# RMSNorm with gamma and Silu on one core: a ring of 24 rows with uneven blocks in place of six equal buffers

## The chip, the cores and the metric

The kernel runs on one core of a Trainium2 chip. The metric is the device time of one execution in microseconds (us). The kernel before was run four times: its median is 316.83 us, the lowest run 316.7 us and the highest 317.09 us.

## What is computed

```python
x = np.random.randn(8, 1024, 2048).astype(np.float32)
gamma = np.random.randn(2048).astype(np.float32)
eps = np.float32(1e-5)

rms = np.sqrt(np.mean(x ** 2, axis=-1, keepdims=True) + eps)
out = gamma * x / rms
return (out * (1 / (1 + np.exp(-out)))).astype(np.float32)
```

The input is 8192 rows of 2048 float32 numbers, 67.11 MB, and the output has the same size. Each row is squared and summed, multiplied by the reciprocal of its root mean square and by gamma, and put through Silu.

## The kernel before

**Tiling.** The 8192 rows are cut into 16 blocks of 512 rows. A block lies in SBUF as 128 partitions of 4 rows (J = 4), each partition's 4 rows being 32 KB that are contiguous in HBM. So the whole problem is 64 "rows per partition" in and 64 out, and below "row" always means one such row over all 128 partitions (1 MB). There are six buffers of 4 rows each (BUFS = 6): 24 rows, 192 KB a partition. All arithmetic is in place: a block is loaded into its buffer, worked on there, and stored from there.

**Queues.** `load` (L52 to L55) issues a block's load from the ScalarE queue (ACTq in the profile; its DMA queue is q10). `store` (L101, L102) issues a block's store from the SyncE queue (SPq; DMA queue q1). Both run on the same 16 DMA engines. The six loads that fill the buffers are issued at the start (L106, L107). A later load, of block b+3, is issued on ScalarE inside the squares of block b+1 (L67 to L69), and goes into the buffer of block b-3, so it waits for that block's store. A store waits for the last Silu of its block.

**Work of a block.** `squares_scalar` squares and sums the first one or two rows on ScalarE (L65, result thrown into PSUM, the sum kept), `squares_vector` the other two or three on VectorE (L73). `root` is a Sqrt on ScalarE with scale and bias (L82), `invert` the reciprocal on VectorE (L87). `multiply` makes x times rstd times gamma in one VectorE instruction for each row (L92). `silu` runs Silu over two rows at a time (L98) and then issues the store.

**Order.** The order of instructions is written out by hand. For most blocks (b from 3 to 13) the squares and the root of block b+1 stand ahead of the product and Silu of block b: a look-ahead of one block. The last block (L149 to L156) is done another way: gamma times x needs no rstd, so the two first products stand ahead of the reciprocal (L152), and the Silu takes rstd as its scale, one row at a time (L154).

**Start.** Gamma is loaded into one partition by SyncE, spread to 128 partitions by TensorE (L114) and copied to SBUF (L115).

Of the kernel before, what the change touches and what calls it, by code (L numbers as in the profile page):

```python
# [1 line left out]

# [4 lines left out]

ACT = mybir.ActivationFunctionType
ALU = mybir.AluOpType


@with_exitstack
def kernel(
    ctx: ExitStack,
    tc: tile.TileContext,
    x: bass.AP,
    gamma: bass.AP,
    eps: bass.AP,
    out: bass.AP,
):  # L20

    nc = tc.nc
    P = nc.NUM_PARTITIONS
    f32 = mybir.dt.float32
    x2 = x.flatten_outer_dims()
    o2 = out.flatten_outer_dims()  # L30
    n, d = x2.shape
    J = 4
    BUFS = 6
    nblk = n // (P * J)
    xb = x2.rearrange("(b p j) d -> b p (j d)", p=P, j=J)
    ob = o2.rearrange("(b p j) d -> b p (j d)", p=P, j=J)

    singles = ctx.enter_context(tc.tile_pool(name="singles", bufs=1))
    pool = ctx.enter_context(tc.tile_pool(name="pool", bufs=BUFS))
    small = ctx.enter_context(tc.tile_pool(name="small", bufs=2))  # L40
    psum = ctx.enter_context(tc.tile_pool(name="psum", bufs=1, space=bass.MemoryType.PSUM))

    Q = 4
    w = d // Q
    g = singles.tile([P, d], f32)
    eps_t = singles.tile([P, 1], f32)
    ones = singles.tile([P, P], f32)
    junk_a = psum.tile([P, d], f32, name="junk_a")
    junk_v = psum.tile([P, d], f32, name="junk_v")
    blocks, sss, rmss, rstds = {}, {}, {}, {}  # L50

    def load(b):  # L52
        xt = pool.tile([P, J * d], f32, name="xt")
        nc.scalar.dma_start(out=xt, in_=xb[b])  # L54
        blocks[b] = xt  # L55

    def row(b, j):
        return blocks[b][:, j * d:(j + 1) * d]

    def squares_scalar(b, loads=()):  # L60


        sss[b] = small.tile([P, J], f32, name="ss")
        for j in range(share(b)):
            nc.scalar.activation(out=junk_a, in_=row(b, j), func=ACT.Square,  # L65
                                 accum_out=sss[b][:, j:j + 1])
            if j == 0:  # L67
                for s in loads:
                    load(s)  # L69

    def squares_vector(b):
        for j in range(share(b), J):
            nc.vector.tensor_tensor_reduce(  # L73
                out=junk_v, in0=row(b, j), in1=row(b, j), scale=1.0, scalar=0.0,
                op0=ALU.mult, op1=ALU.add, accum_out=sss[b][:, j:j + 1])

    def share(b):
        return 1 if 4 <= b <= 12 and b % 2 == 0 else 2

    def root(b):  # L80
        rms = small.tile([P, J], f32, name="rms")
        nc.scalar.activation(out=rms, in_=sss.pop(b), func=ACT.Sqrt, scale=1.0 / d, bias=eps_t)  # L82
        rmss[b] = rms

    def invert(b):
        rstd = small.tile([P, J], f32, name="rstd")
        nc.vector.reciprocal(out=rstd, in_=rmss.pop(b))  # L87
        rstds[b] = rstd

    def multiply(b):  # L90
        for j in range(J):
            nc.vector.scalar_tensor_tensor(out=row(b, j), in0=row(b, j), scalar=rstds[b][:, j:j + 1],  # L92
                                           in1=g, op0=ALU.mult, op1=ALU.mult)

    def silu(b):
        for h in range(0, J, 2):
            cols = slice(h * d, (h + 2) * d)
            nc.scalar.activation(out=blocks[b][:, cols], in_=blocks[b][:, cols], func=ACT.Silu)  # L98
        store(b)

    def store(b):  # L101
        nc.sync.dma_start(out=ob[b], in_=blocks[b])  # L102

    with tc.manual_schedule():

        for b in range(BUFS):  # L106
            load(b)  # L107
        nc.vector.memset(ones, 1.0)  # L108
        nc.vector.memset(eps_t, float(eps))
        nc.scalar.activation(out=junk_a[:, 0:1], in_=ones[:, 0:1], func=ACT.Square)  # L110
        nc.sync.dma_start(out=g[0:1, :], in_=bass.AP(tensor=gamma.tensor, offset=gamma.offset, ap=[[d, 1], [1, d]]))
        for c in range(Q):
            cols = slice(c * w, (c + 1) * w)
            nc.tensor.matmul(junk_v[:, cols], ones[0:1, :], g[0:1, cols], start=True, stop=True)  # L114
        nc.vector.tensor_copy(out=g, in_=junk_v)  # L115

        last = nblk - 1
        SOON = 3  # L120
        squares_scalar(0)
        squares_vector(0)
        root(0)
        invert(0)
        for b in range(last):
            loads = [b + 3] if BUFS <= b + 3 < nblk else []
            if b < SOON:
                multiply(b)
                squares_scalar(b + 1, loads)
                silu(b)  # L130
                squares_vector(b + 1)
                root(b + 1)
            elif b < last - 1:
                squares_scalar(b + 1, loads)
                squares_vector(b + 1)
                root(b + 1)
                multiply(b)
                silu(b)
            else:
                multiply(b)  # L140
                squares_scalar(b + 1)
                silu(b)
                squares_vector(b + 1)
                root(b + 1)
            if b + 1 < last:
                invert(b + 1)


        for j in range(J):  # L149
            if j == J // 2:  # L150
                invert(last)
            nc.vector.tensor_mul(out=row(last, j), in0=row(last, j), in1=g)  # L152
        for j in range(J):
            nc.scalar.activation(out=row(last, j), in_=row(last, j), func=ACT.Silu,  # L154
                                 scale=rstds[last][:, j:j + 1])
        store(last)  # L156


# [1 line left out]
_INS = ['x', 'gamma', 'eps']  # L160
_OUTS = [((8, 1024, 2048), 'float32')]

_NUMBERS = {'eps': 9.999999747378752e-06}


# [26 lines left out]
```

## Time and profile before

| what | value |
|---|---|
| median of four runs | 316.83 us |
| the profiled execution's own time | 317.07 us |
| span that the profile shows of it | 315.3 us |
| VectorE busy | 235.3 us, 75% of the span |
| ScalarE busy | 213.7 us, 68% of the span |
| bytes moved by DMA | 134.24 MB, mean 426 GB/s |
| time that DMA packets took, as a share of 16 engines' span | q10 (loads) 49.8%, q1 (stores) 49.3% |
| median time from issue to landing | loads 38.7 us, stores 29.3 us |

The page gives busy times by engine, then the span in 40 slices with the DMA engines' share and rate in each, the DMA queues, the chain of work that ended last, and the groups of instructions by line. In a group "x60 | 137.0, 2345 | 0.1" says 60 instructions, 137.0 us busy in all, 2345 ns each, and 0.1 us of idle time ahead of them. A DMA "packet" in these counts is either one partition's 32 KB of a block or the four bytes that report a DMA engine's end to a semaphore: a block's DMA has 128 of the first and 16 of the second, 8 and 1 on each of the 16 DMA engines.

### The profile page before, as it was taken

How to read it: one execution, taken by the hardware profiler on the slowest of the kernel's cores; microseconds unless marked ns; L12 is line 12 of the kernel's file. 1: busy time of each engine (PE TensorE's matmuls, PEld its weight loads, DVE VectorE, ACT ScalarE, POOL GpSimd, SP SyncE). 2: the span in 40 equal slices, each digit the busy share in tenths (PEclk: the TensorE clock that was granted, in tenths of full speed). 3: DMA queues.
4: the chain of work that ended last, by engine and by line, in shares of the span. 5: the costliest groups of instructions: out<-in, count | busy, mean ns of one | idle time of the engine just before them, and what ended most of it. 6: DMA issues, size and time to landing. Idle time of an engine off the chain costs nothing.

```text
span 315.3 us, 437 instructions
## 1 busy us (share of the span) xinstructions
PE 7.2 (2%) x8; PEld 2.5 (1%) x8; DVE 235.3 (75%) x157; ACT 213.7 (68%) x136; POOL 0.2 (0%) x4
## 2 busy tenths in 40 slices
PE   6200000000000000000000000000000000000000
PEld 2000000000000000000000000000000000000000
DVE  0579597979995695957969489693996929999600
ACT  1349998972799258782687727876278768779910
POOL 0000000000000000000000000000000000000000
DMA  8999999999999999999999999999999999999996
GB/s 329 416 449 424 403 437 403 466 399 466 399 467 399 463 403 461 403 461 403 461 412 453 416 449 424 445 424 441 432 432 432 432 449 412 457 407 457 407 457 279
DMA packets 4612, 134.24 MB, mean 426 GB/s; under 512 B 513, under 2 KB 513, under 8 KB 513
## 3 DMA queue, kind: packets, MB, share of 16 engines
q10 hardware_dynamic: 2304, 67.11, 49.8%
q1 hardware_dynamic: 2306, 67.12, 49.3%
q14 instruction: 2, 0.02, 0.0%
HBM read 67.12 MB, written 67.11 MB: 426 GB/s over the span
## 4 chain that ended last, share of the span: by engine, by line
DMA 68%; DVE 14%; ACT 11%; issue 2%; ACTq 1%; DVEq 0%
DMA xt<-in_x_dram 68%; DVE xt L92 9%; DVE junk_v L73 5%; ACT xt L98 4%; ACT junk_a L65 3%; ACT xt L154 2%; ACT L82 1%; ACTq L187 1%; ACT L154 0%; ACT L98 0%; ACT rms L82 0%; DVE ss L73 0%; DVE rstd L87 0%; ACTq L54 0%; ACTq L82 0%
## 5 line engine op out<-in xcount | busy, mean ns | idle before, releaser
L92 DVE SCALAR_TENSOR_TENSOR xt<-xt,rstd,g 128x2048 f32<-128x2048 f32 x60 | 137.0, 2345 | 0.1
L98 ACT ACTIVATE xt<-xt 128x4096 f32<-128x4096 f32 x30 | 108.3, 3615 | 27.1 <-DVE xt L92 27.1
L73 DVE CUSTOM_DVE_ANT_0 junk_v<-xt 128x2048 f32<-128x2048 f32 x37 | 85.1, 2299 | 42.9 <-DMA xt<-in_x_dram 42.2
L65 ACT ACTIVATE junk_a<-xt 128x2048 f32<-128x2048 f32 x27 | 50.7, 1876 | 23.1 <-DMA xt<-in_x_dram 22.8
L82 ACT ACT_TABLE_LOAD x15 | 19.2, 1283 | 27.4 <-DVE ss L73 27.3
L98 ACT ACT_TABLE_LOAD x14 | 18.0, 1283 | 0.2
L115 DVE COPY g<-junk_v 128x2048 f32<-128x2048 f32 x1 | 2.3, 2291 | 9.1 <-PE junk_v L114 9.1
L87 DVE RECIPROCAL rstd<-rms 128x4 f32<-128x4 f32 x16 | 2.7, 172 | 8.3 <-ACT rms L82 8.3
L152 DVE TENSOR_TENSOR xt<-xt,g 128x2048 f32<-128x2048 f32 x4 | 8.9, 2278 | 0.0
L82 ACT ACTIVATE rms<-ss,eps_t 128x4 f32<-128x4 f32 x16 | 4.8, 297 | 5.7 <-DVE ss L73 5.5
L154 ACT ACTIVATE xt<-xt,rstd 128x2048 f32<-128x2048 f32 x4 | 7.7, 1990 | 0.0
L114 PE MATMUL junk_v<-g,ones 1*128 1x512 f32 x8 | 7.2, 1072 | 2.9 <-DMA g<-in_gamma_dram 2.9
L73 DVE DVE_READ_ACCUMULATOR2_ANT ss<- 128x1 f32 x37 | 5.2, 140 | 0.0
L65 ACT ACTIVATION_READ_ACCUMULATOR junk_a<-xt 128x1 f32 x27 | 5.0, 186 | 0.0
L110 ACT ACT_TABLE_LOAD x1 | 1.3, 1283 | 3.8 <-issue 3.8
L114 PEld LDWEIGHTS junk_v<-g,ones 1*128 1x128 f32 x8 | 2.5, 327 | 6.0 <-issue 6.0
L154 ACT ACT_TABLE_LOAD x1 | 1.3, 1283 | 0.0
L108 DVE MEMSET ones<- 128x128 f32 x1 | 0.2, 165 | 0.8 <-PEq L173 0.8
L110 ACT ACTIVATE junk_a<-ones 128x1 f32<-128x1 f32 x1 | 0.2, 174 | 0.0
L173 POOL MEMSET const-bfloat16-1.0<- 128x1 bf16 x1 | 0.1, 103 | 0.0
L173 POOL MEMSET const-uint8-127<- 128x1 uint8 x1 | 0.1, 103 | 0.0
L173 POOL MEMSET const-float32-1.0<- 128x1 f32 x1 | 0.1, 100 | 0.0
(2 smaller groups left out, 0.2 us busy)
## 6 DMA issues: line engine op xcount, KB each, us to landing
xt<-in_x_dram ACTq DMA_DIRECT2D x16, 4096.0 KB, 38.7
out_dram<-xt SPq DMA_DIRECT2D x16, 4096.0 KB, 29.3
g<-in_gamma_dram SPq DMA_DIRECT2D x1, 8.0 KB
```

The costliest lines, as they stand in the source:

```text
L65: nc.scalar.activation(out=junk_a, in_=row(b, j), func=ACT.Square, accum_out=sss[b][:, j:j + 1])
L73: nc.vector.tensor_tensor_reduce(out=junk_v, in0=row(b, j), in1=row(b, j), scale=1.0, scalar=0.0, op0=ALU.mult, op1=ALU.add, accum_out=sss ...
L82: nc.scalar.activation(out=rms, in_=sss.pop(b), func=ACT.Sqrt, scale=1.0 / d, bias=eps_t)
L87: nc.vector.reciprocal(out=rstd, in_=rmss.pop(b))
L92: nc.vector.scalar_tensor_tensor(out=row(b, j), in0=row(b, j), scalar=rstds[b][:, j:j + 1], in1=g, op0=ALU.mult, op1=ALU.mult)
L98: nc.scalar.activation(out=blocks[b][:, cols], in_=blocks[b][:, cols], func=ACT.Silu)
L110: nc.scalar.activation(out=junk_a[:, 0:1], in_=ones[:, 0:1], func=ACT.Square)
L114: nc.tensor.matmul(junk_v[:, cols], ones[0:1, :], g[0:1, cols], start=True, stop=True)
L115: nc.vector.tensor_copy(out=g, in_=junk_v)
L152: nc.vector.tensor_mul(out=row(last, j), in0=row(last, j), in1=g)
L154: nc.scalar.activation(out=row(last, j), in_=row(last, j), func=ACT.Silu, scale=rstds[last][:, j:j + 1])
L187: with _tile.TileContext(nc) as tc:
```

## The change

The six buffers become one ring tile of 24 rows per partition. The 64 rows are cut into 12 blocks of 4, 4, 6, 4, then seven times 6, then 4 rows; a block of 6 rows is 48 KB a partition, contiguous in HBM. The first five blocks fill the ring (4 + 4 + 6 + 4 + 6 = 24); from there blocks 5 to 10 go to the places 0, 6, 12, 18, 0 and 6, and block 11 to place 12. Load i+2 is issued on ScalarE behind the first Silu row of block i, for i from 3 to 9; it waits for the stores of the blocks whose rows it overwrites, the youngest of which is block i-2.

Each block is done by itself, with no instruction of the next one between: half its rows squared on ScalarE and half on VectorE, the root, then gamma products of two rows at a time with no rstd in them (the reciprocal behind the first pair), then Silu by rows with rstd as scale, then the store. On VectorE the order is: the block's squares, first pair, reciprocal, other pairs, and then the next block's squares. On ScalarE: the block's squares, Sqrt, all its Silu rows, and then the next block's squares. The first pair of products overwrites rows that ScalarE squares, so it waits for those squares.

```diff
-    J = 4
-    BUFS = 6
-    nblk = n // (P * J)
-    xb = x2.rearrange("(b p j) d -> b p (j d)", p=P, j=J)
-    ob = o2.rearrange("(b p j) d -> b p (j d)", p=P, j=J)
+    RING = 24
+    sizes = [4, 4, 6, 4] + [6] * 7 + [4]
+    R = max(sizes)
+    nblk = len(sizes)
+    starts, places = [], []
+    row, place = 0, 0
+    for k in sizes:
+        if place + k > RING:
+            place = 0
+        starts.append(row)
+        places.append(place)
+        row, place = row + k, place + k
+    first = next(i for i in range(1, nblk) if places[i] == 0)
+
+    def block(t, i):
+        lo, k = starts[i] * P, sizes[i]
+        return t[lo:lo + k * P, :].rearrange("(p r) d -> p (r d)", r=k)
...
-    pool = ctx.enter_context(tc.tile_pool(name="pool", bufs=BUFS))
+    ring = singles.tile([P, RING * d], f32)
...
+    def rows(i, lo, hi):
+        return ring[:, (places[i] + lo) * d:(places[i] + hi) * d]
+
+    def load(i):
+        nc.scalar.dma_start(out=rows(i, 0, sizes[i]), in_=block(x2, i))
+
+    def store(i):
+        nc.sync.dma_start(out=block(o2, i), in_=rows(i, 0, sizes[i]))
+
+    def compute(i):
+        k = sizes[i]
+        mid = k // 2
...
+        for r in range(mid):
+            nc.scalar.activation(out=junk_a, in_=rows(i, r, r + 1), func=ACT.Square,
+                                 accum_out=ss[:, r:r + 1])
+        for r in range(mid, k):
             nc.vector.tensor_tensor_reduce(
-                out=junk_v, in0=row(b, j), in1=row(b, j), scale=1.0, scalar=0.0,
-                op0=ALU.mult, op1=ALU.add, accum_out=sss[b][:, j:j + 1])
+                out=junk_v, in0=rows(i, r, r + 1), in1=rows(i, r, r + 1), scale=1.0, scalar=0.0,
+                op0=ALU.mult, op1=ALU.add, accum_out=ss[:, r:r + 1])
+        nc.scalar.activation(out=rms[:, 0:k], in_=ss[:, 0:k], func=ACT.Sqrt, scale=1.0 / d, bias=eps_t)
+        for r in range(0, k, 2):
+            if r == 2:
+                nc.vector.reciprocal(out=rstd[:, 0:k], in_=rms[:, 0:k])
+            two = rows(i, r, r + 2).rearrange("p (r d) -> p r d", r=2)
+            nc.vector.tensor_mul(out=two, in0=two, in1=g.unsqueeze(1).to_broadcast([P, 2, d]))
+        for r in range(k):
+            row = rows(i, r, r + 1)
+            nc.scalar.activation(out=row, in_=row, func=ACT.Silu, scale=rstd[:, r:r + 1])
+            if r == 0 and i + 2 in range(first, nblk):
+                load(i + 2)
+        store(i)
...
-        for b in range(BUFS):
-            load(b)
+        for i in range(first):
+            load(i)
...
-        last = nblk - 1
-        SOON = 3
-        squares_scalar(0)
-        squares_vector(0)
-        root(0)
-        invert(0)
-        for b in range(last):
...
-        store(last)
+        for i in range(nblk):
+            compute(i)
```

More of the change, by code (lines that the diff above doesn't have):

```diff
@@ L49 @@
     junk_v = psum.tile([P, d], f32, name="junk_v")
[L50 to L69, printed above, removed]
@@ L71, in squares_vector @@
-    def squares_vector(b):
-        for j in range(share(b), J):
-            nc.vector.tensor_tensor_reduce(
-                out=junk_v, in0=row(b, j), in1=row(b, j), scale=1.0, scalar=0.0,
-                op0=ALU.mult, op1=ALU.add, accum_out=sss[b][:, j:j + 1])
[L77 to L99, printed above, removed]
@@ L101, in store @@
-    def store(b):
-        nc.sync.dma_start(out=ob[b], in_=blocks[b])
+    def rows(i, lo, hi):
[7 more added lines that the diff above has]
+        mid = k // 2
+        ss = small.tile([P, R], f32, name="ss")
+        rms = small.tile([P, R], f32, name="rms")
+        rstd = small.tile([P, R], f32, name="rstd")
+        for r in range(mid):
+            nc.scalar.activation(out=junk_a, in_=rows(i, r, r + 1), func=ACT.Square,
+                                 accum_out=ss[:, r:r + 1])
+        for r in range(mid, k):
+            nc.vector.tensor_tensor_reduce(
+                out=junk_v, in0=rows(i, r, r + 1), in1=rows(i, r, r + 1), scale=1.0, scalar=0.0,
[12 more added lines that the diff above has]
+        store(i)
@@ L112 @@
         for c in range(Q):
-            cols = slice(c * w, (c + 1) * w)
-            nc.tensor.matmul(junk_v[:, cols], ones[0:1, :], g[0:1, cols], start=True, stop=True)
+            nc.tensor.matmul(junk_v[:, c * w:(c + 1) * w], ones[0:1, :], g[0:1, c * w:(c + 1) * w],
+                             start=True, stop=True)
         nc.vector.tensor_copy(out=g, in_=junk_v)
-        last = nblk - 1
-        SOON = 3
-        squares_scalar(0)
-        squares_vector(0)
-        root(0)
-        invert(0)
-        for b in range(last):
[L126 to L155, printed above, removed]
-        store(last)
+        for i in range(nblk):
+            compute(i)
 _INS = ['x', 'gamma', 'eps']
```

## The prediction

> **What bounds the kernel now.** I read the page's engine shares and DMA slices first, then the DMA queues, the chain that ended last, and the DMA queues in short stretches. First the page:
>
> ```profile
> PE 7.2 (2%) x8; PEld 2.5 (1%) x8; DVE 235.3 (75%) x157; ACT 213.7 (68%) x136; POOL 0.2 (0%) x4
> ...
> DMA  8999999999999999999999999999999999999996
> ...
> q10 hardware_dynamic: 2304, 67.11, 49.8%
> q1 hardware_dynamic: 2306, 67.12, 49.3%
> ```
>
> No compute engine is near full, while the DMA engines are busy in every slice but the first and last: loads and stores together fill 99.1% of them. Taken over one stretch, from the first bytes to the last:
>
> ```profile
> 1.20:312.90 311.70, 7.16 (x8) 2.50 (x8) 235.12 (x155) 213.74 (x136) 0.00 (x0) 1.00 1.00 431
> ```
>
> The last three columns are clock, DMA share and GB/s: share 1.00. So 311.7 of the 315.3 us are DMA without a hole, 1.2 us lie ahead and 2.4 behind. Every idle time of an engine is slack under that. The chain agrees: 68% of it is a load, and its ScalarE and VectorE pieces lie beside busy DMA engines.
>
> Next, how fast DMA goes and how two queues share it. From the timeline (start, duration, then what ended the idle time):
>
> ```profile
> 13.26 1.88 ACT L65 ACTIVATE junk_a<-xt 128x2048 f32<-128x2048 f32 x1 [8.04 <-DMA xt<-in_x_dram]
> 13.31 2.30 DVE L73 CUSTOM_DVE_ANT_0 junk_v<-xt 128x2048 f32<-128x2048 f32 x1 [0.93 <-DMA xt<-in_x_dram]
> ...
> 22.89 1.88 ACT L65 ACTIVATE junk_a<-xt 128x2048 f32<-128x2048 f32 x1 [3.16 <-DMA xt<-in_x_dram]
> ...
> 24.92 1.88 ACT L65 ACTIVATE junk_a<-xt 128x2048 f32<-128x2048 f32 x1
> ```
>
> Blocks 0 and 1 land 9.63 us apart: 8 packets on each DMA engine, 1.204 us each. Later, with both queues busy (the chain's loads from 104.72 to 182.35), two blocks in and two out take some 38.8 us, 1.21 us a packet. Now the queues in one microsecond and in the next:
>
> ```profile
> q1 hardware_dynamic: 10, 0.33, 75.8%
> q10 hardware_dynamic: 6, 0.20, 45.5%
> ...
> q10 hardware_dynamic: 10, 0.33, 75.8%
> q1 hardware_dynamic: 6, 0.20, 45.5%
> ```
>
> Ten packets take 75.8% of 16 us: 1.213 us each, as long as a packet of loads alone (143 of them, 127 of 32 KB, fill 100.4% of 16 engines from 13.2 to 22.8 us). A packet isn't stretched by the other queue; each engine serves one packet of one queue, then one of the other. This matters below, since the change makes packets of 48 KB and of 32 KB.
>
> **The change, part by part.**
>
> *Bytes and DMAs.* The bytes stay: 64 rows in, 64 out. The DMAs go from 32 to 24; on each DMA engine 256 data packets become 64 of 32 KB and 128 of 48 KB. A 48 KB packet is in no row. If a packet's time is all bytes, it takes 1.82 us and the sum is unchanged: 0. If the 9 ns between 1.213 and 1.204 are a fixed cost, 64 packets fewer save 0.6 us. On the other side, the nearest row of a DMA loss is where stores first join the loads:
>
> ```profile
> 35.00:38.00 3.00, 0.00 (x0) 0.00 (x0) 0.96 (x2) 2.97 (x4) 0.00 (x0) 1.00 1.26 481
> 38.00:42.00 4.00, 0.00 (x0) 0.00 (x0) 4.00 (x3) 3.95 (x5) 0.00 (x0) 1.00 0.75 279
> ```
>
> Mean (3x481 + 4x279)/7 = 366 GB/s against 432: 1.1 us lost, once. Were such a loss paid at each of the eight places where a queue goes from one packet size to the other or starts, it would be 8.8 us; nothing shows that size is its cause. I take -0.3, the middle of the two nearer ends, and keep +2.2 (two such losses) for the range.
>
> [...]
>
> *Engine work.* VectorE loses the 60 products with rstd (137.0 us) and gets 32 products of pairs, each by the two-row stretch of L152 4.5 us: 32 x 4.5 = 144, where 137.0 + 8.9 stood. Silu by rows is 64 x 1.92 (7.68/4 of L154) = 123 where 108.3 + 7.7 stood. Table loads go from 31 to 25, 1.28 each. All of it is under the DMA as long as no queue runs dry, so its cost is 0; what it costs without that cover depends on how long a block takes, without look-ahead:
>
> - Block ready, ScalarE frees last: squares of rows 0 and 1, 2 x 2.03 (13.26 to 15.29 is one) = 4.1; first pair 4.5, for it overwrites those rows; reciprocal 0.2 (Sqrt and its table load end before); then one pair (4 rows) or two (6 rows) of 4.5; two Silu 3.9. Sum 17.2 for 4 rows, 21.7 for 6.
> - Block just landed: VectorE's own squares come first, 2.39 each (13.31 to 15.70): 4.8 or 7.2 in place of 4.1, sums 17.9 and 24.8.
>
> DMA needs 6 x 2 x 2.42 = 29.1 us for six rows in and out, so the engines keep up. What the look-ahead hid is now latency between landing and store; who notices is the store queue, if it is empty then.
>
> *Does a queue run dry?* I follow the packets, 8 per block and engine (1.213 or 1.82), one from each queue in turn, 1.2 us from last packet to landing.
> - Store 0 is issued at 13.3 + 4.8 + 4.5 + 0.2 + 4.5 + 3.9 = 31.2 (before: 35.4) and starts near 32.4. Block 2's last 2.1 packets pass with 2.1 of it: 2.1 x 3.03, to 38.8.
> - Block 3, 8 x 2.43, to 58.2. Store 0 ends at 53.1; store 1 is issued at 31.2 + 17.2 = 48.4, 4.7 ahead.
> - Block 4 beside store 1's last 5.9 packets, 5.9 x 3.03, to 76.1; store 2 came at 48.4 + 21.7 = 70.1, 6.0 ahead. Then 2.1 x 3.64: block 4 ends at 83.7.
> - Load 5 needs store 1 (77.3) and Silu row 0 of block 3 (about 80): in time for 83.7. Loads 5 and 6 end at 111.6 and 137.1 by the same steps, stores 2 and 3 at 105.2 and 129.5.
> - From there all blocks have 6 rows, 8 x 3.64 = 29.1 us each. Load i+2 goes out when store i-2 has landed, some 6 us before the load ahead of it ends.
> - End: load 10 ends at 253.6, load 11 at 277.9. Then stores run alone: 9 to 288.6, 10 to 303.2, 11 to 312.9. Store 10 is ready at 253.6 + 1.2 + 24.8 = 279.6, store 11 at some 297.5: 9 and 6 us ahead.
>
> No gap: DMA ends at 312.9 as before.
>
> *The added wait.* Load i+2 stands on ScalarE behind the first Silu row and waits there for store i-2: block 6's Silu begins at 138.3 + 7.2 + 4.5 + 0.2 = 150.2, store 4 lands at 158.6 + 1.2. Behind it on ScalarE wait five Silu rows (9.8 us) and the block's store, ready at 169.6, while store 5 runs until 187.7. Cost 0. If store 5 were gone by then, DMA would still have the load.
>
> Sum: 315.3 + 0 - 0.3 = 315.0 us of span. The profiled run took 317.07, 0.24 over the median; the same 0.3 off the median gives 316.5.
>
> [...]
>
> **Rivals.**
> *1. Sharing by bytes* (slower). If 48 KB goes out at half rate beside 32 KB, the early 6-row loads lose their larger share, loads end later and fewer stores are left to cover the last blocks. From 32.4 on 51.6 rows remain to load at 4.84: to 282.1. Load 10 lands near 263.9, store 10 is issued at 288.7, while store 9 has ended at 282.1 + 2.4 x 2.42 = 287.9: with 1.3 to start 2.1 us idle. It ends at 304.5; store 11 comes at 288.7 + 17.2 + 1.3 = 307.2: 2.7 idle. Sum +4.8: 321.3. It decides once store 10 or 11 comes after its predecessor's end. For it: no row shows packets of two sizes. Against it: the packets' unstretched 1.213 us. Chance 0.14.
> *2. Size-change losses* (slower): two more of the 1.1 us losses, 316.5 + 2.2 = 318.7. The one loss seen is at a change of the mix, but the last change, to stores alone near 280, shows none. 0.10.
> *3. The wait on ScalarE drains both queues.* Each of some six steady blocks would pay the start of a load, 12.4 (first load, issue to landing) - 9.7 = 2.7: +16, 333. The 6 us and 18 us of cover above speak against it. 0.04.
> *4. Larger packets pay* (faster): the whole 0.6 and part of the 38-to-42 loss, together 1.1: 315.7. Against it: 1.204 is already reached with 32 KB. 0.12.
>
> **How the numbers follow.** The forecast, DMA without a hole, has 0.60, own range 315.9 to 317.4. About 0.2%, 0.63 us, is what a measurement here can tell from no change: of the 0.60, 0.06 is faster and 0.02 slower than that. Faster 0.06 + 0.12 = 0.18, same 0.52, slower 0.02 + 0.14 + 0.10 + 0.04 = 0.30. The range goes from 315.2 (rival 4 and its lower half) to 320.4 (rival 2, and rival 1 with part of its idle time); about 0.17 is left out, nearly all above.
>
> **What would show it.** DMA share 1.00 from 1.2 to 312.9 again; store 0 issued near 31.2; 48 KB packets of 1.82 us; loads ended near 278 and last store issued near 297. Wrong: a DMA hole near 288 or 305 (rival 1), loads ended after 281, or a rate below 425 GB/s in slices with both queues busy (rival 2).

## The result, and the profile after

| | kernel before | changed kernel |
|---|---|---|
| median | 316.93 us (62 runs) | 317.36 us (43 runs) |
| lowest and highest run | 316.70 and 317.19 us | 316.88 and 319.46 us |
| the profiled execution: time, span | 317.07, 315.3 us | 317.13, 315.3 us |

The changed kernel takes 1.0019 times as long, with a 95% interval of 1.0015 to 1.0024: some 0.6 us more, where 0.3 us less was forecast (the ratio is one of means; the medians are 0.43 us apart). The time lies inside the stated range of 315.2 to 320.4 us; what came out the other way is the direction. Two things stand out. The loss is small but certain, and the changed kernel scatters over 2.6 us where the kernel before scatters over 0.5 us. The profiled execution happens to be one of its quicker runs, with the same span as before, so it shows the course of the kernel well and the loss badly; the loss is looked for in the other profiles below.

The page after, with the lines that were shown of before:

```profile
PE 7.2 (2%) x8; PEld 2.5 (1%) x8; DVE 217.1 (69%) x111; ACT 222.9 (71%) x166; POOL 0.2 (0%) x4
...
DMA  8999899999999999999999999999999999999996
...
q10 hardware_dynamic: 1728, 67.11, 49.6%
q1 hardware_dynamic: 1730, 67.12, 49.2%
```

VectorE has 18 us less to do and ScalarE 9 us more, and DMA is busy in every slice as before. The same bytes go in 25% fewer packets (64 data packets fewer and 8 end marks fewer on each of the 16 DMA engines), and the packets take 98.8% of the span instead of 99.1%. The one stretch from the first bytes to the last (length, busy time of PE, PE's weight loads, VectorE, ScalarE and GpSimd, then clock, DMA share and GB/s) is again full:

```profile
1.20:312.90 311.70, 7.16 (x8) 2.49 (x8) 216.90 (x109) 222.88 (x166) 0.00 (x0) 1.00 1.00 431
```

The prediction's schedule can be read off the timeline of the changed kernel: the issue of store 0, the first instruction on block 4, load 6's issue and the Silu rows that waited behind it, the first instructions on blocks 5, 6 and 11, and the last store's issue.

```profile
30.58 0.36 SPq L69 DMA_DIRECT2D out_dram<-ring  x1
...
85.18 1.88 ACT L79 ACTIVATE junk_a<-ring 128x2048 f32<-128x2048 f32 x1 [0.16 <-DMA ring<-in_x_dram]
...
106.86 0.34 ACTq L66 DMA_DIRECT2D ring<-in_x_dram  x1
107.25 9.57 ACT L93 ACTIVATE ring<-ring,rstd 128x2048 f32<-128x2048 f32 x5 [8.51 <-DMA out_dram<-ring]
112.94 2.30 DVE L82 CUSTOM_DVE_ANT_0 junk_v<-ring 128x2048 f32<-128x2048 f32 x1 [7.61 <-DMA ring<-in_x_dram]
...
138.92 2.30 DVE L82 CUSTOM_DVE_ANT_0 junk_v<-ring 128x2048 f32<-128x2048 f32 x1 [4.99 <-DMA ring<-in_x_dram]
...
279.40 2.30 DVE L82 CUSTOM_DVE_ANT_0 junk_v<-ring 128x2048 f32<-128x2048 f32 x1 [4.02 <-DMA ring<-in_x_dram]
...
296.78 0.33 SPq L69 DMA_DIRECT2D out_dram<-ring  x1
```

| event | forecast, us | trace, us |
|---|---|---|
| store 0 issued | 31.2 | 30.58 |
| block 4 landed | 83.7 + 1.2 = 84.9 | 85.18 |
| block 5 landed | 111.6 + 1.2 = 112.8 | 112.94 |
| block 6 landed | 137.1 + 1.2 = 138.3 | 138.92 |
| block 11 landed | 277.9 + 1.2 = 279.1 | 279.40 |
| last store issued | 297.5 | 296.78 |

Nothing in this table is off by more than 0.8 us in 300. The view of waits has the wait that the change put on ScalarE (us in total, times, longest):

```profile
ACT ring L93 <- DMA out_dram<-ring: 47.0, 6, 8.7
```

Six waits, none over 8.7 us, and no hole in DMA beside any of them. How one DMA engine shares itself between a queue with 48 KB packets (block 3 or 4 loading) and one with 32 KB (block 0 going out) stands in the queues from 35 to 38 us:

```profile
q10 hardware_dynamic: 16, 0.79, 60.5%
q1 hardware_dynamic: 16, 0.52, 40.4%
```

Sixteen packets of each. 60.5% of 16 engines' 3 us is 29.0 us, 1.815 us a packet of 48 KB, and 40.4% is 19.4 us, 1.212 us a packet of 32 KB. By the single records each of the 16 engines has one packet of either queue in these 3 us, and from 45 to 270 us 2364 of 2384 records (end marks counted) follow one of the other queue on their engine. So an engine turned from one queue to the other after each single packet here, and the queue with the larger packets got the larger share.

So the schedule, the share and the packet price were as forecast, and yet the kernel is slower. What is left is the end. The last queue lines of four profiles, from 313 us on (packets that start after 313 us, MB, share of 16 engines; the four bytes that each engine writes as the end mark of the last store count as a packet). Before:

```profile
q1 hardware_dynamic: 16, 0.00, 0.2%
```

The changed kernel, the profiled execution above:

```profile
q1 hardware_dynamic: 7, 0.00, 0.1%
```

The changed kernel once more, run as the first experiment, at 318.57 us:

```profile
q1 hardware_dynamic: 9, 0.10, 4.6%
```

And as the last one, at 317.72 us:

```profile
q1 hardware_dynamic: 9, 0.03, 1.6%
```

Before, all 16 engines write their end marks after 313 us, and no packet of data starts any more. In the three executions of the changed kernel eight to ten engines are already done by then, but in the two slower ones packets of data still start: three of 32 KB (0.10 MB, on two engines) and one (0.03 MB). The typical engine became quicker, and in those two the slowest one slower.

### The profile page after: what moved, and what is told of

Same layout as the page of the kernel before. It is cut to its first block, busy times and chain, and to the rows that moved or that the text cites. A ratio compares the mean times of both kernels' runs of the same rounds, so it can differ in the third digit from the quotient of the medians.

```text
span 315.3 us, 402 instructions
## 1 busy us (share of the span) xinstructions
PE 7.2 (2%) x8; PEld 2.5 (1%) x8; DVE 217.1 (69%) x111; ACT 222.9 (71%) x166; POOL 0.2 (0%) x4
## 4 chain that ended last, share of the span: by engine, by line
DMA 59%; DVE 18%; ACT 14%; issue 2%; ACTq 1%; DVEq 0%
DMA out_dram<-ring 45%; DVE ring L90 15%; DMA ring<-in_x_dram 14%; ACT ring L93 12%; ACT junk_a L79 3%; DVE junk_v L82 2%; ACTq L142 1%; ACTq L66 0%; DVE rstd L88 0%; DVE ss L82 0%; DVEq L142 0%; DVEq L82 0%
## 5 line engine op out<-in xcount | busy, mean ns | idle before, releaser
L93 ACT ACTIVATE ring<-ring,rstd 128x2048 f32<-128x2048 f32 x64 | 124.0, 1992 | 58.0 <-DMA out_dram<-ring 47.0
L90 DVE TENSOR_TENSOR ring<-ring,g 128x4096 f32<-128x4096 f32 x32 | 140.4, 4407 | 8.0 <-ACT junk_a L79 8.0
L82 DVE CUSTOM_DVE_ANT_0 junk_v<-ring 128x2048 f32<-128x2048 f32 x32 | 73.6, 2299 | 58.1 <-DMA ring<-in_x_dram 57.5
L79 ACT ACTIVATE junk_a<-ring 128x2048 f32<-128x2048 f32 x32 | 60.0, 1875 | 9.1 <-DMA ring<-in_x_dram 8.4
L79 ACT ACTIVATION_READ_ACCUMULATOR junk_a<-ring 128x1 f32 x32 | 6.0, 186 | 0.0
L82 DVE DVE_READ_ACCUMULATOR2_ANT ss<- 128x1 f32 x32 | 4.5, 140 | 0.0
L85 ACT ACTIVATE rms<-ss,eps_t 128x6 f32<-128x6 f32 (+1 forms) x12 | 3.6, 299 | 0.1
L88 DVE RECIPROCAL rstd<-rms 128x6 f32<-128x6 f32 (+1 forms) x12 | 2.1, 178 | 0.0
```

The lines of the kernel that those rows point to most:

```text
L79: nc.scalar.activation(out=junk_a, in_=rows(i, r, r + 1), func=ACT.Square, accum_out=ss[:, r:r + 1])
L82: nc.vector.tensor_tensor_reduce(out=junk_v, in0=rows(i, r, r + 1), in1=rows(i, r, r + 1), scale=1.0, scalar=0.0, op0=ALU.mult, op1=ALU.ad ...
L85: nc.scalar.activation(out=rms[:, 0:k], in_=ss[:, 0:k], func=ACT.Sqrt, scale=1.0 / d, bias=eps_t)
L88: nc.vector.reciprocal(out=rstd[:, 0:k], in_=rms[:, 0:k])
L90: nc.vector.tensor_mul(out=two, in0=two, in1=g.unsqueeze(1).to_broadcast([P, 2, d]))
L93: nc.scalar.activation(out=row, in_=row, func=ACT.Silu, scale=rstd[:, r:r + 1])
```

## The experiments

All kernels compute the whole reference; some load bytes or square rows whose result nobody uses, as told at each. Each number is a median, with lowest and highest run and the count behind it, then the ratio to the kernel before on the same chip with its 95% interval. The changed kernel's own helper names are used in the diffs (`rows`, `block`, `sizes`); `junk_a` is the PSUM tile into which results are thrown.

**1. The changed kernel again**, and once more beside the last set, without an edit.

> The changed kernel as it is, once more, as the control of its set. All theories: a median some 0.2% over the kernel before, 317.2 to 317.6 us, single times from 316.9 to 319. Theory A (stray long load packets make the 16 DMA engines drift apart): the profile shows every packet slot filled from 1.2 to about 312 us again, and the four-byte end marks of the last store spread by more than the 0.95 us that the kernel before shows, by an amount that changes from one execution to the next. Theory B (the load's wait on ScalarE or the late last stores leave DMA engines empty): a hole of 0.5 us or more in the DMA share between 140 and 300 us.

> The changed kernel alone, the control of this set: 317.2 to 317.8, scatter over 1 us, 5 to 10 stretched load packets (over 60 ns) behind 100 us.

Measured: 317.80 us (317.25 to 318.58, 11), 1.0026 [1.0016, 1.0035]; and 317.43 us (317.01 to 319.33, 12), 1.0020 [1.0009, 1.0031]. The loss and the scatter come back.

**2. Is it the arithmetic?** The kernel before, with its loads, stores and look-ahead, but with products of pairs of rows without rstd and with Silu by rows scaled by rstd.

```diff
-        for j in range(J):
-            nc.vector.scalar_tensor_tensor(out=row(b, j), in0=row(b, j), scalar=rstds[b][:, j:j + 1],
-                                           in1=g, op0=ALU.mult, op1=ALU.mult)
+        for j in range(0, J, 2):
+            two = blocks[b][:, j * d:(j + 2) * d].rearrange("p (r d) -> p r d", r=2)
+            nc.vector.tensor_mul(out=two, in0=two, in1=g.unsqueeze(1).to_broadcast([P, 2, d]))
...
-        for h in range(0, J, 2):
-            cols = slice(h * d, (h + 2) * d)
-            nc.scalar.activation(out=blocks[b][:, cols], in_=blocks[b][:, cols], func=ACT.Silu)
+        for j in range(J):
+            nc.scalar.activation(out=row(b, j), in_=row(b, j), func=ACT.Silu, scale=rstds[b][:, j:j + 1])
```

> The kernel before with the change's arithmetic alone: products with gamma in pairs without rstd, Silu row by row with rstd as scale. Blocks, buffers, look-ahead and DMAs stay. The forecast's reading (engine work lies under the DMA): 316.9, same within 0.1%. If the arithmetic costs: up to 317.4.

Measured: 317.16 us (317.01 to 317.76, 11), 1.0008 [1.0000, 1.0017]. The arithmetic costs at most 0.5 us and most likely some 0.2 us. That alone doesn't rule it out as a part of the loss; experiment 6 has the same arithmetic at 1.0005.

**3. Who shares how?** The blocks of 6 rows go as a DMA of 4 rows and one of 2 (32 and 16 KB packets), in both directions. That sets the old share back for part of the time.

```diff
+    def pieces(t, i):
+        r = 0
+        while r < sizes[i]:
+            k = min(4, sizes[i] - r)
+            lo = (starts[i] + r) * P
+            yield r, r + k, t[lo:lo + k * P, :].rearrange("(p r) d -> p (r d)", r=k)
+            r += k
...
-        nc.scalar.dma_start(out=rows(i, 0, sizes[i]), in_=block(x2, i))
+        for lo, hi, src in pieces(x2, i):
+            nc.scalar.dma_start(out=rows(i, lo, hi), in_=src)
```

(the same in `store`, on SyncE)

> A block of 6 rows moved as a DMA of 4 rows and a DMA of 2 rows, each contiguous in HBM: packets of 32 and 16 KB at distances of 32 and 16 KB, 320 on each engine. If the queues take turns packet by packet (the forecast's reading), the 6-row loads lose their larger share beside 4-row stores, loads end later and the last two stores come too late: holes of some 5 to 6 us near 290 and 305, and 128 x 0.009 = 1.2 us for packets: 322.5 to 324.5. If the queues share by bytes, only the 1.2: 318.5. If the 48 KB distance makes the scatter, single times lie within 0.5 us of each other; if the order of work makes it, they spread as the changed kernel's.

Measured: 323.98 us (322.24 to 328.99, 5), 1.0209 [1.0188, 1.0230]. The stretches near its end (the columns are those of the one-stretch view above):

```profile
300.00:305.00 5.00, 0.00 (x0) 0.00 (x0) 5.00 (x3) 3.33 (x3) 0.00 (x0) 1.00 0.88 374
305.00:310.00 5.00, 0.00 (x0) 0.00 (x0) 1.24 (x1) 4.58 (x3) 0.00 (x0) 1.00 0.00 0
310.00:315.00 5.00, 0.00 (x0) 0.00 (x0) 0.00 (x0) 0.17 (x1) 0.00 (x0) 1.00 0.98 419
```

DMA stands still for over 5 us in all while ScalarE and VectorE finish the last block. That is the hole of rival 1. Its cause is an estimate, worked out from the packets in turn: loads get a smaller share, end later, and the stores that should cover the last block's arithmetic have gone out already. Following the packets one by one in turn put it there before the run, at 322.5 to 324.5 us; some 1.2 us of the loss was to be the fixed cost of the added packets.

**4. Smaller packets with the same blocks.** Each load and each store goes as two DMAs of half the rows: 24 and 16 KB packets.

```diff
-        nc.scalar.dma_start(out=rows(i, 0, sizes[i]), in_=block(x2, i))
+        h = sizes[i] // 2
+        for r in (0, h):
+            nc.scalar.dma_start(out=rows(i, r, r + h), in_=block(x2, i)[:, r * d:(r + h) * d])
```

> Each load and store as two DMAs of half the rows: packets of 24 and 16 KB in place of 48 and 32 KB, 384 on each engine in place of 192. Order, block places and HBM rows per partition stay, and so does the 6 to 4 ratio of packet sizes, so the queues share as in the changed kernel. A fixed cost of 9 ns a packet (3 x 1213 - 2 x 1815 ns in the profile after) makes it 192 x 0.009 = 1.7 us slower: lowest time 318.6 in place of 316.9. If the scatter comes from the length of a packet, it falls below +-0.3 us; if from the 48 KB distance between partitions in HBM, or from the order of work, it stays 1 us or more.

Measured: 317.56 us (317.45 to 317.92, 11), 1.0022 [1.0013, 1.0030]. The lowest run is 1.1 us under what was expected, and the scatter is gone. Its packets take 912 and 611 ns, so the fixed part is 3 x 611 - 2 x 912 = 9 ns again. The expectation made 192 x 9 ns = 1.7 us of that; the median engine in fact ends 1.3 us later than in the changed kernel (314.21 against 312.92 us, table below). That this one isn't slower than the changed kernel means that the changed kernel loses over a microsecond elsewhere, which this one doesn't lose.

**5. All blocks of 4 rows** in the ring, with loads three ahead, as before.

```diff
-    sizes = [4, 4, 6, 4] + [6] * 7 + [4]
+    sizes = [4] * 16
...
-            if r == 0 and i + 2 in range(first, nblk):
-                load(i + 2)
+            if r == 0 and i + 3 in range(first, nblk):
+                load(i + 3)
```

> The changed kernel's order of work (no look-ahead, products in pairs, Silu by rows) with 16 blocks of 4 rows and load i+3 behind the first Silu row of block i, as far ahead as in the kernel before. All packets have 32 KB. Theory A with 48 KB packets as its cause: 316.9, the kernel before's time, within 0.3, with its small scatter (all within 0.5 us). If the order of work without look-ahead is what costs: 317.4 or more, with single times up to 319. If the packets' fixed cost is the only thing that differs from the changed kernel's best runs (316.9): 317.5.

Measured: 322.56 us (322.17 to 323.73, 4), 1.0185 [1.0167, 1.0203]. A miss of all theories: 5 us slower with the packets of before, the order of the changed kernel and only a small hole (1.2 us near 307 us). The queues from 131 to 136 us, at the end of a store that comes 3.8 us behind the end of a load (132.7 and 128.9 us, medians of the engines' end marks):

```profile
q10 hardware_dynamic: 40, 1.31, 64.9%
q1 hardware_dynamic: 38, 0.72, 33.5%
```

Forty load packets of 32 KB take 64.9% of 80 us: 1.30 us each, not 1.213. Single load packets are stretched here, and such bursts come back at each block: by the single records 131 load packets after 100 us, 34 us in all, which is 2.1 us for each engine. That gave a new theory: what matters is how far apart on the engines the ends of loads and of stores lie, which the time of store 0 sets once for the whole run.

**6. The same with store 0 later.** Three squares of gamma, thrown into PSUM, stand ahead of the last Silu row of block 0, so that store 0 is issued near 36 us instead of 30.6.

```diff
         for r in range(k):
+            if i == 0 and r == k - 1:
+                for _ in range(3):
+                    nc.scalar.activation(out=junk_a, in_=g, func=ACT.Square)
             row = rows(i, r, r + 1)
```

> The kernel of e4_all_four (all blocks of 4 rows, changed order; 322.56) with three squares of gamma on ScalarE ahead of the last Silu row of block 0, whose result is thrown away: store 0 goes out near 36 us in place of 30.6, as in the kernel before (35.4). Nothing else differs. Theory C: load packets are stretched when a store's end meets a load's start on the engines (in e4_all_four the bursts of long load packets, 0.2 to 0.6 us each, lie at the ends of stores, some 2 us behind the ends of loads; in the kernel before the ends lie 6 us apart and there are none): 317 +- 0.5, long packets gone. If the order of work or the three pairs of engines' accesses to SBUF stretch them: still 322 or more.

Measured: 317.14 us (316.96 to 317.65, 11), 1.0005 [0.9997, 1.0014]. Three useless instructions take 5.4 us off. Loads now end 4.8 us behind stores, and no load packet after 100 us is stretched. The same view of this kernel, 131 to 136 us:

```profile
q1 hardware_dynamic: 33, 1.08, 50.1%
q10 hardware_dynamic: 33, 1.08, 50.0%
```

Load packets are back at 50.0% of 80 us by 33, 1.212 us. This kernel has the changed kernel's ring, its order within a block and its arithmetic, with blocks of 4 rows, loads three ahead and a later store 0, and it costs nothing that can be told against before. So none of these has to cost anything, and what is left of the change is its blocks of 6 rows, and the time of store 0, which experiment 8 moves.

**7. One engine alone.** The kernel before, with ten loads of 6 KB into one partition behind stores 3 to 12. Such a load has one packet, on one of the 16 engines (in the page's q1 line below the ten add 20 packets to the 2306 of before: ten of 6 KB and ten end marks); its data is used by nobody.

```diff
     def store(b):
         nc.sync.dma_start(out=ob[b], in_=blocks[b])
+        if 3 <= b < 13:
+            nc.sync.dma_start(out=extra, in_=x2[0:1, 0:1536])
```

> The kernel before, with ten loads of 6 KB into one partition behind the stores of blocks 3 to 12 (data nobody uses). Each is one packet on one DMA engine, some 0.24 us: 2.4 us of work for one of the 16 engines, 0.15 us of the mean of all. If the slowest engine sets the end (the reading of the changed kernel's scatter): 318.3 to 319.3, that engine's end 1.6 to 2.4 us behind the median engine's. If engines share what is left: 317.0 to 317.2.

Measured: 319.95 us (319.26 to 320.27, 4), 1.0089 [1.0076, 1.0102]. Ten packets, 0.06 MB of 134, cost 3.0 us, which is 0.6 us more than their own 2.4 us (an estimate: 9 ns and 6 x 37.6 ns each, from the packets of 16 to 48 KB that were measured) and above the range that was expected; why it is more stays open. The page's queue lines and the first line of its chain:

```profile
q10 hardware_dynamic: 2304, 67.11, 49.4%
q1 hardware_dynamic: 2326, 67.18, 49.0%
...
DMA 67%; DVE 14%; ACT 11%; issue 2%; ACTq 1%; SPq 0%
```

and its queue from 313 us on:

```profile
q1 hardware_dynamic: 17, 0.07, 3.2%
```

0.07 MB: two packets of 32 KB start after 313 us, both on the one late engine; the other engines have no data left and take none of it over. The mean share of all 16 hardly moves (49.4% and 49.0% where 49.8% and 49.3% stood), and the kernel ends with the one that is late: its end mark comes at 316.16 us, 2.92 us behind the median engine's.

With that, each profile's last end marks are the thing to read. From the trace's single DMA records, in us of the span (stretched: load packets after 100 us that took over 60 ns more than their size's usual time, with the time over it):

| kernel | packets, KB | median engine ends | last engine ends | lag | stretched, us |
|---|---|---|---|---|---|
| before | 32 | 313.34 | 314.10 | 0.75 | 1, 0.24 |
| before with the new arithmetic (2) | 32 | 313.27 | 314.22 | 0.95 | 0 |
| blocks of 4, store 0 later (6) | 32 | 313.26 | 314.48 | 1.22 | 0 |
| halves (4) | 24, 16 | 314.21 | 314.56 | 0.35 | 0 |
| changed, the profiled one | 48, 32 | 312.84 | 314.10 | 1.25 | 6, 1.40 |
| changed, 317.72 us | 48, 32 | 313.02 | 314.59 | 1.57 | 10, 2.20 |
| changed, 318.57 us | 48, 32 | 312.90 | 315.45 | 2.54 | 8, 1.98 |
| one engine alone (7) | 32 | 313.24 | 316.16 | 2.92 | 0 |

The span ends 1.2 to 1.4 us after the last engine in each. Of the 24 stretched packets in the changed kernel's rows 18 have 48 KB and six have 32 KB (loads of the last block). The three executions of the changed kernel have a mean median engine at 312.92, 0.37 us earlier than the mean of the first three rows (313.29), which is most of the gain that the packets were to bring; their mean lag is 1.79 us against 0.97, 0.82 more. The difference, +0.45 us, is that between these six executions; that it lies near the +0.6 of all runs fits, but six single executions, some of them the slow ones of their kernel, don't prove it.

What makes the last engine late can be followed further. On an engine each packet's record starts 3 or 4 ns before the one ahead of it ends, so the records fall into 16 chains. In the kernel before, the last engine met a load of instructions (queue q14, 8 KB), which with the longer packet behind it took 0.67 us, and one stretched load packet (0.24): lag 0.75. In the profiled execution of the changed kernel it met a load of instructions with a longer packet behind it (0.84; that packet is one of the six in the table) and three more stretched load packets (0.54): lag 1.25. At 318.57 us it met two loads of instructions with their packets (0.85), three stretched load packets from 85 us on (0.85), and it had lost 1.75 us where the stores join the loads, from 32 to 38 us, where the median engine lost 0.65: lag 2.54. So stretched load packets are a part of the lag; loads of instructions, which the kernel before has too, and the join are others.

**8. Do stores join the loads at a bad place?** In the changed kernel store 0 joins beside 48 KB packets. First, sizes that let it join beside 32 KB:

```diff
-    sizes = [4, 4, 6, 4] + [6] * 7 + [4]
+    sizes = [4, 4, 4] + [6] * 8 + [4]
```

> The changed kernel with blocks of 4, 4, 4, eight times 6, and 4 rows: as many packets of each size, but the stores join the loads while 32 KB packets are loaded, as in the kernel before, and not 48 KB ones. Following the packets gives the same time to 0.1 us. If the changed kernel's late DMA engine gets its delay mostly at that join (0.4 to 1.6 us a packet there in the profiles of the changed kernel, 0.2 to 0.85 in the kernel before), the median comes down to 316.5 to 316.9 and the scatter under 0.6 us. If the delay comes from stray packets in the steady part, median 317.3 to 317.8 and scatter 1.3 us or more as before.

Measured: 319.17 us (317.94 to 321.61, 6), 1.0066 [1.0044, 1.0089]. Its premise failed: by 32.7 us, when store 0 started, block 3 with its 48 KB packets had begun. What it shows is another thing, in the stretch near the end:

```profile
305.00:310.00 5.00, 0.00 (x0) 0.00 (x0) 0.00 (x0) 1.69 (x1) 0.00 (x0) 1.00 0.56 239
```

One late engine let the last block land late, so its store was issued late (the last load's end marks come at 284.0 us on the median engine and at 289.0 on the last), and by the single records most of the other engines idled for some 3.5 us, from 304.1 to 307.6. After 100 us 41 of its load packets are stretched, by 10.3 us in all. So a lag before the last load ends can also cost time on the engines that aren't late.

Then the changed kernel with store 0 later, by three squares and by one, as in 6.

> The changed kernel with three squares of gamma on ScalarE (result thrown away) ahead of block 0's last Silu row: store 0 starts near 37 us, when 32 KB packets of block 3 are loaded and not the 48 KB ones of block 2, and in the steady part loads end some 3.5 packet pairs behind the ends of stores in place of 2. Bytes and packets stay. If the join of the first store with 48 KB loads (and what it does to one engine) is what makes the changed kernel's slow engine: 316.4 to 316.9, scatter under 0.6 us, the packets' 0.3 to 0.6 us kept. If the stray delays come from instruction loads and steady packets: 317.2 to 317.8, scatter over 1 us.

> The same with one such square: store 0 starts near 33.7 us, still beside 48 KB packets of block 2, and loads end 1.5 packet pairs behind the ends of stores. If the join with 48 KB packets matters: as the changed kernel, 317.3 to 317.8. If the distance between ends of loads and stores matters (in e4_all_four and e5_join_on_four the ends lie close and the time is 319 to 322): between the two, 317.5 to 319. If neither: 317.4.

Measured: 318.17 us (317.21 to 319.97, 11), 1.0042 [1.0026, 1.0059]; and 317.99 us (317.59 to 319.15, 6), 1.0040 [1.0028, 1.0052]. Neither is faster than the unedited one (1.0019 in 43 runs, 1.0026 [1.0016, 1.0035] in experiment 1), where one theory had the first faster than the kernel before; the first lies above both of its ranges. A join beside 48 KB packets isn't needed for the loss, though what an engine loses at the join can add to its lag, as the execution at 318.57 us shows.

**9. Ten blocks of 6 rows and one of 4**, with no mix of sizes until the end, and the same with store 0 later.

```diff
-    sizes = [4, 4, 6, 4] + [6] * 7 + [4]
+    sizes = [6] * 10 + [4]
```

> The changed kernel with ten blocks of 6 rows and one of 4: all packets but the last block's have 48 KB, 176 on each engine in place of 192 (0.14 us less by 9 ns each); block 0 lands 4.8 us later, store 0 goes out near 42. By the packets alone 0.3 us under the changed kernel's best: 316.6. With the strays as in the changed kernel: 317.2 to 317.6. If blocks whose ends come close make it worse (loads end 1.5 pairs behind stores): up to 319.

> e11_six with three squares of gamma ahead of block 0's last Silu row: loads end 3.5 packet pairs behind stores. If that distance keeps strays away: 316.3 to 316.7 with scatter under 0.6 us, under the kernel before. If it doesn't matter: as e11_six.

Measured: 324.24 us (322.09 to 325.17, 5), 1.0204 [1.0182, 1.0227]; and 317.28 us (316.95 to 318.66, 12), 1.0023 [1.0013, 1.0034]. The time of store 0 is worth 7 us here too, and the first kernel lies far above the 319 us that were expected at most. The distance of the ends is not the reason here: after 100 us loads end 9.7 us behind stores in the first and 7.2 us in the second. The queues from 60 to 70 us, of the first:

```profile
q1 hardware_dynamic: 43, 2.11, 55.4%
q10 hardware_dynamic: 35, 1.72, 45.3%
```

and of the second:

```profile
q10 hardware_dynamic: 47, 2.31, 53.3%
q1 hardware_dynamic: 45, 2.21, 51.0%
```

In the first a packet of either queue takes some 2.06 us in place of 1.815: its loss begins in the 50 us behind the start of store 0, in loads and stores. The second one scatters like the changed kernel. Its profiled run (316.95 us) has ten stretched load packets, 2.34 us, spread over seven engines; nine of them fell on engines that were not last, and the lag is 0.44 us. That fits a scatter that comes from the luck of which engine they fall on.

**10. Does a 48 KB kernel make more of a late engine?** Three loads of 6 KB as in 7, behind stores 0 to 2, in the kernel before, in the changed one and in the halves of 4.

```diff
+        if b < 3:
+            nc.sync.dma_start(out=extra, in_=x2[0:1, 0:1536])
```

> The kernel before with three loads of 6 KB into one partition behind stores 0 to 2 (data nobody uses): one DMA engine gets three packets of 0.24 us, 0.73 us in all. The engine ends 0.73 us later than it would; no stretched load packets in the steady part: 317.2 to 317.7, scatter under 0.6 us.

> The changed kernel with the same three loads. If an engine out of step gets its 48 KB packets stretched, the 0.73 us grow to 1.5 us or more: 318.2 to 319.5 with stretched load packets on the engine that has the small loads. If strays fall on engines by chance, the push adds 0.73 at most: 317.4 to 318.1.

> The kernel of e2_halves (the changed kernel's order, packets of 24 and 16 KB; 317.56) with the same three loads. If long packets are what stretches: the push adds its 0.73 us at most, 317.8 to 318.3, scatter under 0.6 us. If the changed order of work or the 48 KB distance between partitions is: 318.5 to 320.

Measured: before 319.00 us (317.50 to 319.32, 6), 1.0057 [1.0041, 1.0073], which is 2.1 us more than without them; changed 318.10 us (317.64 to 318.37, 5), 1.0035 [1.0023, 1.0047], 0.67 more; halves 318.21 us (318.08 to 318.38, 5), 1.0041 [1.0028, 1.0054], 0.65 more than the halves of experiment 4 (on another chip). The theory that 48 KB packets make an engine's lateness grow falls: the changed kernel pays for the three loads no more than the halves do. The kernel before pays three times as much; in its trace store packets were stretched by 1.9 us in all between 89 and 100 us, which no theory had foreseen.

No version beat the kernel before.

## Why the prediction was wrong, point by point

**"Bytes and DMAs", the step that failed.** Its value was -0.3 us, the middle of the two nearer ends, 0 and -0.6; measured were +0.6. A fixed cost of a packet is real: 3 x 1213 - 2 x 1815 = 9 ns from the changed kernel itself, the same 9 ns from the halves. That the prediction had 9 ns too is luck: it took them from 1.213 us, a packet's time, and 1.204 us, an eighth of the time between two landings, both of 32 KB packets, which can't tell a fixed part; and it said itself that a packet of loads alone takes 1.213 us. By the records 64 packets fewer save 0.58 us of packet time, but 0.37 us at the median engine's end, which fits each packet starting 3 or 4 ns before the one ahead of it ends (64 x 3.5 ns are 0.22 us). What was missing is a term on the other side. The step went from the sum of packets to the end of the kernel as if 16 engines were one, and the trace's DMA share of 1.00, a mean over 16, hid that they are not: the kernel ended with the slowest engine (in each profile of the table the span ends 1.2 to 1.4 us behind that engine's end mark; experiment 7), and in the three profiled executions of the changed kernel the slowest one was 0.8 us further behind than in the three with 32 KB packets alone (the table), which more than takes back the 0.37 us. The step did keep +2.2 as an end, by stores joining the loads; the size covers what happened, the mechanism doesn't. The kernel before had the trace of it already: its last engine's end mark comes 0.75 us after the median one's.

**"Engine work", cost 0.** Right as to the cover: no queue ran dry, and the new arithmetic alone cost 0.1% [0.0, 0.2] in the old kernel (experiment 2).

**"Does a queue run dry?"** Right, event by event (the table of the result). What it took from the trace, one packet from each queue in turn at a price by bytes, is the part of the work that held.

**"The added wait", cost 0.** Right: waits of at most 8.7 us where the prediction's times for block 6 give 7.7 (from the end of the first Silu row, near 152.1, to 159.8), behind which nothing on DMA stood still. Blocks of 4 rows with the same kind of wait cost nothing against before (experiment 6).

**Rival 1, sharing by bytes**, is refuted by the 16 and 16 packets of 35 to 38 us. The hole near the end that it foresaw appears when the loads lose their larger packets (experiment 3).

**Rival 2, size-change losses.** The sign came out, the reason did not: moving the join brought no gain (experiment 8), the median engine lost no more at the join than before (0.69 us in the profiled execution, 0.76 before), and a kernel with no change of size until its end scatters as much (experiment 9).

**Rival 3** did not happen. **Rival 4, larger packets pay**, is true of the median engine and not of the kernel.

**What would show it.** The share of 1.00, store 0, 1.82 us and the ends of loads and stores all came as listed, and the kernel was slower nevertheless. The list watched means and the schedule; it had no line for the last engine.

**What stays open.** Why load packets are stretched now and then in the kernels with 48 KB packets: six to ten of them after 100 us in each of the seven profiles of experiments 1, 8 (the last two), 9 (the second), 10 (the changed kernel) and of the result, 1.2 to 2.7 us in all. The length of the load packet itself isn't what singles them out: of these 56, 45 have 48 KB and 11 have 32 KB, which is about one in a hundred of either size, where the three kernels with 32 KB packets alone in the table have one in some 3500. The halves, with the same blocks in packets of 24 and 16 KB, have none. Open too is why the time of store 0 stretches packets of any size in some kernels. That the blocks of 6 rows are the cause of the loss is what is left after the other parts were tried. The link from their packets to the lag rests on counts and ends, not on a run that takes the stretching alone away: the halves take it away, but change the packets' number too.

## What to carry to other kernels

When DMA is full, read the end mark of each DMA engine, not the mean share: here the median engine gained 0.37 us in the profiled executions, the kernel lost 0.6 us over all runs, and ten loads of 6 KB on one engine cost 3.0 us. Before trusting a loss or a gain of one per cent in a kernel that streams in and out, move the first store by a few microseconds: that alone was worth 5 to 7 us in two of these kernels, some ten times the loss under study. Fewer and larger packets saved some 6 ns each at the median engine's end in these kernels (0.37 us for 64 fewer, 1.3 us for the 192 of experiment 4), so from 16 to 48 KB there was little to win by size.

## What the runs showed of the hardware

- Two queues shared a DMA engine by packets: in the changed kernel from 35 to 38 us 16 packets of 48 KB took 60.5% beside 16 of 32 KB with 40.4%; with blocks of 4 rows (experiment 6) from 131 to 136 us 33 of 32 KB took 50.0% beside 33 with 50.1%.
- A packet of 16, 24, 32 and 48 KB took 611, 912, 1213 and 1815 ns: 9 ns and 37.6 ns a KB (1024 bytes). On one engine a packet's record started 3 or 4 ns before the one ahead of it ended.
- Ten packets of 6 KB on one engine cost 3.0 us of a kernel that moves 134 MB.
- Store 0 some 5 us later took 322.56 us to 317.14 with blocks of 4 rows and 324.24 to 317.28 with blocks of 6. With blocks of 4, stores ended 2.8 to 3.9 us behind loads in the slow one, and 131 load packets after 100 us were stretched, by 0.26 us on the mean; in the quick one loads ended 4.8 us behind stores, and none was. With blocks of 6 the ends lay 9.7 and 7.2 us apart, so the distance of the ends is not the rule in general.
- In each profile of the table two or three loads of instructions (8 KB, 309 to 315 ns) go through single DMA engines after the start, and the packet behind one took 107 to 529 ns more than its usual time.
